# Second mixer's latents projected without their norm, which enters in the heads; q's norm in the exponential; c loaded as 32 rows

## Chip, cores and metric

One core of one Trainium2 chip runs the whole kernel in one launch. The metric is device time in microseconds (us). The kernel before takes 999.2 us, the median of three runs (997.95 to 1000.5).

## What is computed

The reference is a trunk of two layers for one sequence of 256 tokens with 1024 features, all in fp32. Each layer is a gated feed-forward network (FFN, 2816 hidden), an attention mixer, and another FFN. Each of these normalizes its input and shifts, scales and gates it with vectors that come from the conditioning vector c. The second mixer projects to a small latent for q (384 wide) and one for k and v (256 wide, and 32 more for a shared rotary part of k), normalizes the latents, and projects them up to 16 heads of 96 (64 without and 32 with rotary position). Cut to what matters here:

```python
def rms_norm(x, g):
    return x * lax.rsqrt(jnp.mean(x * x, axis=-1, keepdims=True) + EPS) * g

def mla_shared_kv(...):
    hs = modulate(rms_norm(x, kv_norm_g), shift, scale)   # shift, scale from silu(c)
    ckv_kpe = hs @ w_dkv
    ckv = rms_norm(ckv_kpe[..., :256], kv_a_norm_g)
    kpe = ckv_kpe[..., 256:]
    k_nope = (ckv @ w_uk).reshape(B, S, 16, 64)
    v = (ckv @ w_uv).reshape(B, S, 16, 64)
    k = concatenate([k_nope, kpe for every head])
    k = rms_norm(k, k_g)                    # over 96, then rope on the last 32
    return k, v

def mla_attention(h, ...):
    q = (rms_norm(h @ w_dq, q_a_norm_g) @ w_uq).reshape(B, S, 16, 96)
    q = rms_norm(q, q_g)                    # over 96, then rope on the last 32
    o = causal_attention(q, k, v, scale=96 ** -0.5)
    return o.reshape(B, S, 1024) @ w_o
```

A root-mean-square norm divides each row by a number of its own. A row of the latent that is not divided by it gives a row of q (or k, v) that is too large by that number, and the norm over the head divides it out again, up to the small constant EPS, which must then be multiplied by the square of that number.

## The kernel before

The 256 tokens are two tiles of 128, called t. Every fp32 product with a weight is three matmuls: the weight is split into a rounded part hi (written by ScalarE, L634) and a rest lo (written by VectorE, L635), and so is the activation (`split_evac`, L779 and L780); the products hi·hi, hi·lo and lo·hi are summed in PSUM (`mm3`, L764 to L766). Weights come by DMA on SyncE's queue in one long stream.

The stages run in this order: `first` (the start and the first 768 hidden rows of the first FFN, until about 52 us), the rest of the first FFN, the first mixer (about 240 to 340), two FFNs, the second mixer `mla` (about 704 to 804), and the last FFN. The conditioning weights (16 tiles of 512 KB for each norm, and as many halves for the gates) are multiplied with c on VectorE (L645 for shifts and scales, L683 for gates) all through the kernel; L645 multiplies a tile of weights with `c_b`, which is c, after SiLU, repeated on all 128 partitions.

The order of the instructions on each engine is not that of the program. The class `Order` records all instructions with their dependencies, gives each a cost from formulas (`duration`) and each buffer pool its number of buffers, places the instructions by list scheduling in a simulated time, and then fixes the order found, engine by engine. `later(us, fn)` in the program text postpones the emission of a piece of work by that much estimated TensorE time; constants such as `LAT_WAIT` are such waits. So a change of one instruction, cost or constant can move instructions anywhere in the kernel.

The start. The queue of ScalarE loads c (as 128 partitions by 8 columns, L1523) and then `cols` (biases, gains and other columns, L1524). SyncE's queue loads x and then the first weights. ScalarE applies SiLU to c (L1536). Eight matmuls (L1541, sixteen passes in the profile) repeat c on all partitions: the stationary operand is a column of c broadcast to 128 columns, the moving one is the identity; the result is copied in two halves to `c_b` (L1542). For the norm of x, VectorE takes the square sum of tile 0 (L1558), ScalarE that of tile 1 (L1555), GpSimd takes the power −0.5 (L801), and ScalarE puts it on a diagonal (L1562), by which TensorE transposes and scales x at once (L1572). With the shift and scale from L645, ScalarE makes z (L1589), which is split to h, and the main matmuls follow (L1609 to L1611), for k from 0 to 7 with the weights rounded by L1600 and L1601. Matmuls of zeros into the accumulators (L1548) open them and run before all of this.

The second mixer. For each t, TensorE projects to the q latent and to the k-v latent. `lat_norm_T` (L1376) takes ScalarE's square sum of a latent from PSUM (L1379), adds EPS on VectorE (L1381), takes the power −0.5 on GpSimd (L1383), multiplies the latent from PSUM by that and by the gain on VectorE (L1384), and later transposes it on TensorE (L1389) and splits it to `qlT` or `ckT` (L779, L780). Then four groups g of four heads: `proj` projects the latent to q, `head_rstd` (L1103) takes square (ScalarE, L1106), sum by head (VectorE, L1109), add (L1110) and power (GpSimd, L1111), VectorE multiplies (L1474, `qn`), and the rotary part follows. k and v are done the same way (L1488, L1489, L1491). `to_T` (L1449) transposes q and k on TensorE, four heads at a time for each t (L1454), into a tile of the pool `ps_tr`, which has three PSUM banks and also serves the latents' transposes, the scores, the transposed probabilities and the output; ScalarE copies each with the gain (L1455). `attention` then makes scores in three units: a mask by a matmul (L1018) with the products of q and k on top (L1020), the negated maximum on VectorE (L1030), the exponential on ScalarE (L1041), reciprocal and multiplication on VectorE (L1046, L1047), transposes of the probabilities (L1056) with ScalarE's copies (L1058), and the products with v (L1076). `out_proj` closes the mixer. The pool `ps_ada` has one PSUM bank, which the gates' sums use.

Of the kernel before, what the change touches and what calls it, by code (L numbers as in the profile page):

```python
# [21 lines left out]
P = 128  # L22
D = 1024
KD = D // P
# [42 lines left out]
AV_WAIT = 2.6  # L67
LAT_WAIT = 5.0
G_WAIT = 2.6
# [59 lines left out]
def lay_out(v):  # L129
# [54 lines left out]
WAKE = 100.0  # L184
SWITCH = 95.0
TABLE = 1280.0
RATE = 330.0
# [59 lines left out]
class Order:  # L247
# [120 lines left out]
    def place(self, need):  # L368
# [68 lines left out]
        while placed < n:  # L437
# [90 lines left out]
def trunk(ctx: ExitStack, tc: tile.TileContext, a: dict, out: bass.AP):  # L528
# [88 lines left out]

    all_cols = cp.tile([P, 3 * NK + NT + 4 + 2 * RO], F32, name="cols")
    cact = cp.tile([P, KD], F32, name="cact")
    places = {}  # L620
    c0 = 3 * NK
    for name, n in (("pos", NT), ("moba_q", 1), ("moba_k", 1), ("q", 1), ("q_pe", RO), ("k", 1), ("k_pe", RO)):
        places[name] = all_cols[:, c0:c0 + n]
        c0 += n
    cols = all_cols[:, :3 * NK].rearrange("p (i c) -> p i c", i=3)
    m_cols = cp.tile([P, 2, NK], F32, name="m_cols")
# [375 lines left out]

    def attention(ap, g, qTs, kTs, vs, bias, oT, state, after_s=None):

# [5 lines left out]
        def scores():  # L1010
# [14 lines left out]
            for (t, es), ps3 in zip(UNITS, banks):  # L1025
                nk = P * (t + 1)
                s3 = ap.tile([P, 512], F32, tag="w", name=nm("s"), bufs=5).rearrange("p (e k) -> p e k", k=nk)
                mx = small([P, 4], "mx")
                if bias is None:
                    nc.vector.tensor_reduce(mx[:, :len(es)], ps3, axis=AX.X, op=ALU.max, negate=True)  # L1030
                else:
                    for i, e in enumerate(es):
                        s2, ps2 = [x[:, i, :].rearrange("p (b c k) -> p b c k", c=P // NB, k=NB) for x in (s3, ps3)]
                        nc.vector.tensor_tensor_reduce(s2, ps2, bias(t, e), 1.0, 3.0e38,
                                                       op0=ALU.add, op1=ALU.min, accum_out=mx[:, i:i + 1])
                ss.append(s3)
                mxs.append(mx)
            for u, (t, es) in enumerate(UNITS):
                sm = small([P, 4], "sm")
                for i in range(len(es)):  # L1040
                    nc.scalar.activation(ss[u][:, i, :], (banks if bias is None else ss)[u][:, i, :], AF.Exp,  # L1041
                                         bias=mxs[u][:, i:i + 1], scale=1.0 if bias is None else -1.0,
                                         accum_out=sm[:, i:i + 1])
# [58 lines left out]

    def head_rstd(ap, src, n, d, extra=None):  # L1103
# [3 lines left out]
        nh = n // (d if extra is None else DH)  # L1107
        v, v2, r = [small([P, 2 * GH], g)[:, :nh] for g in ("hv", "hv2", "hr")]
        nc.vector.tensor_reduce(v, sq.rearrange("p (h d) -> p h d", h=nh), axis=AX.X, op=ALU.add)  # L1109
        nc.vector.tensor_scalar(v2, v, EPS if extra is None else extra, None, op0=ALU.add)  # L1110
        nc.gpsimd.tensor_tensor(r, v2, mhalf[:, :nh], op=ALU.pow)  # L1111
        return r
# [262 lines left out]

    def lat_norm_T(ap, src, n, gain, lat, t):  # L1376
        y = ap.tile([P, 512], F32, tag="w", name=nm("ly"), bufs=5)[:, :n]
        s = small([P, 1], "ssq0")
        nc.scalar.activation(y, src, AF.Square, scale=n ** -0.5, accum_out=s)  # L1379
        v = small([P, 1], "var")  # L1380
        nc.vector.tensor_scalar(v, s, EPS, None, op0=ALU.add)  # L1381
        r = small([P, 1], "rstd")
        nc.gpsimd.tensor_tensor(r, v, mhalf[:, 0:1], op=ALU.pow)  # L1383
        nc.vector.scalar_tensor_tensor(y, src, r, gain, op0=ALU.mult, op1=ALU.mult)  # L1384

        def fin():
# [6 lines left out]
            lat[2].add(t)  # L1393
        later(LAT_WAIT, fin)

    def mla(h, hs, after):
        with ExitStack() as st:
# [10 lines left out]
            qlT = [one([P, QL // P, S], f"qlT{i}", F32R) for i in range(2)] + [set()]  # L1408
            kpr, spe = [], []

            NV = KVL + RO
            pls = [[], []]
            for t in range(NT):
                for i, (src, n) in ((1, (h, QL)), (0, (hs, NV))):
# [5 lines left out]
                    if i:  # L1420
                        lat_norm_T(ap, ps[:, :QL], QL, ga_q, qlT, t)
                        continue
                    lat_norm_T(ap, ps[:, :KVL], KVL, ga_kv, ckT, t)
                    kpe = one([P, 1, RO], f"kpe{t}")
# [24 lines left out]
            def to_T(g, kind, nat, gcol, then):  # L1449
                dst = ap.tile([QK, GH, S], F32, tag=kind + "T", name=nm(kind + "T"))  # L1450
                for t in range(NT):
                    pt = tr_tile()
                    for e in range(GH):
# [6 lines left out]
                if len(then) == 2:  # L1460
                    qT, kT = then["q"], then["k"]
                    attention(ap, g, lambda e, t: qT[:, e, t * P:(t + 1) * P], lambda e, n: kT[:, e, :n],
                              lambda e, kb: vs[g][:, kb, e * DH:(e + 1) * DH], None, oT, state)

            vs = {}
            for g in range(NG):
                then = {}
                pq = nextw()
                qn = ap.tile([P, NT, GH, QK], F32, tag="qn", name=nm("qn"), bufs=1)
                for t in range(NT):  # L1470
# [3 lines left out]
                    nc.vector.tensor_tensor(qn[:, t], heads(pq_), r[:, :, None].to_broadcast([P, GH, QK]), op=ALU.mult)  # L1474
                pes = qn[:, :, :, DH:]
# [7 lines left out]
                for t in range(NT):  # L1483
                    ps = proj(t, ckT, pkv, KVL // P, 2 * GH * DH)
                    until(lambda: state.get("Tk", 0) >= g)
                    pk_ = ps[:, :GH * DH]
                    r = head_rstd(ap, pk_, GH * DH, QK, extra=spe[t])
# [9 lines left out]
    def first(units):  # L1497
# [5 lines left out]
        with ExitStack() as st:  # L1503
            fp = st.enter_context(tc.tile_pool(name="fp", bufs=1))
            zeros = fp.tile([P, P], BF16, name="zeros")
            nc.vector.memset(zeros, 0.0)
            wt = [[splitp.tile([P, D], F32, tag=g, name=nm("adaw")) for g in ("hi", "lo")] for _ in range(KD)]
            cuts = (0, FIRST_A, n1)
# [13 lines left out]
            with ranked(0):  # L1522
                nc.scalar.dma_start(cact, a["c"])  # L1523
                nc.scalar.dma_start(all_cols, a["cols"])  # L1524
# [10 lines left out]
            with ranked(0):  # L1535
                nc.scalar.activation(cact, cact, AF.Silu)  # L1536
                for i in range(2):
                    pt = tr_tile()
                    for j in range(4):
                        k = 4 * i + j  # L1540
                        nc.tensor.matmul(kslice(pt, j), cact[:, k:k + 1].to_broadcast([P, P]), ident, start=True, stop=True)  # L1541
                    nc.scalar.activation(c_b[:, i * 512:(i + 1) * 512], pt, AF.Copy)  # L1542
            ps_x = [tr_tile(), ps_ada.tile([P, 512], F32, tag="ada", name=nm("tr"))]
            accs = [tr_tile() if f >= 4 else mm_tile() for f in range(B1)]


            for f in range(B1):
                nc.tensor.matmul(accs[f], zeros, zeros[:, None].to_broadcast([P, 4, P]), start=True, stop=False)  # L1548
            diag, rs, y, fill = [], [], {}, 10
# [113 lines left out]
```

## Time and profile before

| | before |
|---|---|
| median of the runs | 999.2 us (997.95, 999.2, 1000.5) |
| profiled execution, its own time | 999.38 us |
| span of its instructions | 997.6 us |
| mean granted TensorE clock | 0.997 |
| instructions | 15253 |
| HBM read | 255.34 MB, 260 GB/s over the span |

The span is the time from the first to the last instruction that the profiler saw; 1.8 us of the execution's own time lie outside it. PE is TensorE's matmul stream and PEld its loading of stationary operands beside it, DVE is VectorE, ACT is ScalarE, POOL is GpSimd and SP is SyncE; an engine's name with a q is its queue of DMA issues. A row of the timeline gives start and duration in us, then engine, line and operation, with the operands out<-in; in square brackets stands how long the engine had been idle before and what released it. A row of a group gives busy time and the mean of one in ns, and behind the second bar the idle time before them. The length of a matmul includes its way through the array: where matmuls follow each other, their starts, not their lengths, tell the price.

### The profile page before, as it was taken

To read this page: it belongs to the slowest core of one execution; us is meant where nothing else is said; L and a number is where in the kernel's file an instruction comes from. 1 tells how busy PE (TensorE), PEld (TensorE's weight loads), DVE (VectorE), ACT (ScalarE), POOL (GpSimd) and SP (SyncE) were. 2 spreads that over 40 slices of the span, in tenths; PEclk is the share of its full clock that TensorE was granted. 3 is DMA by queue.
4 is the path that set the end of the run, shared out by engine and by line. 5 is a ranking of instruction groups with operands and counts; after the bars stand their busy time and mean duration, and the time that the engine had idled before them with its cause. 6 is when DMAs were issued, how large, how long until landed. Compare 5 with 4: busy or idle time off the path is not lost.

```text
span 997.6 us, 15253 instructions
## 1 busy us (share of the span) xinstructions
PE 982.7 (99%) x5570; PEld 839.4 (84%) x5570; DVE 845.7 (85%) x1430; ACT 629.9 (63%) x1173; POOL 88.8 (9%) x124
## 2 busy tenths in 40 slices
PE   7999999999999999999999999999999999999998
PEld 6988888888888788888888888888888878888886
DVE  6999999898999899999789999964998789777542
ACT  5689565378766976665367666643879696667421
POOL 1012020022231100000000000000143010000000
PEclk8999999999999999999999999999999999999999
DMA  9978889898786689988979988862343468544530
GB/s 366 404 244 286 312 314 353 311 339 336 261 317 233 226 303 327 340 292 302 371 297 330 353 308 307 286 236 102 106 154 127 169 230 290 199 169 170 230 127 22
DMA packets 53371, 260.53 MB, mean 261 GB/s; under 512 B 6320, under 2 KB 6832, under 8 KB 35120
## 3 DMA queue, kind: packets, MB, share of 16 engines
q1 hardware_dynamic: 51696, 255.93, 70.3%
q0 software_dynamic: 1024, 3.17, 1.1%
q8 instruction: 44, 0.72, 0.3%
q10 hardware_dynamic: 576, 0.45, 0.2%
q14 instruction: 31, 0.25, 0.1%
HBM read 255.34 MB, written 4.19 MB: 260 GB/s over the span
## 4 chain that ended last, share of the span: by engine, by line
PE 91%; DVE 3%; issue 2%; DMA 2%; ACT 1%; POOL 1%; POOLq 0%; ACTq 0%; DVEq 0%
PE mm L964 23%; PE mm L764 15%; PE mm L765 15%; PE mm L766 15%; PE mm L972 12%; PE at L1020 2%; DMA bias_d<-bt 1%; PE at L1076 1%; PE at L1056 1%; PE tr L814 1%; PE mm L1609 1%; DVE lo L635 1%; PE mm L1610 1%; PE mm L1611 1%; PE tr L1454 1%
## 5 line engine op out<-in xcount | busy, mean ns | idle before, releaser
L635 DVE TENSOR_TENSOR lo<-raw,hi 128x1024 fp32r<-128x1024 f32 (+3 forms) x312 | 369.0, 1199 | 69.6 <-ACT hi L634 64.2
L634 ACT ACTIVATE hi<-raw 128x1024 fp32r<-128x1024 f32 (+3 forms) x312 | 319.6, 1038 | 154.3 <-PE mm L766 117.4
L964 PE MATMUL mm<-h,hi 128*128 128x512 f32 x1120 | 289.2, 394 | 1.1 <-DVE g L903 0.8
L964 PEld LDWEIGHTS mm<-h,hi 128*128 128x128 f32 x1120 | 199.5, 189 | 36.5 <-DVE g L903 1.6
L972 PEld LDWEIGHTS mm<-h,lo 128*128 128x128 f32 x1120 | 155.3, 190 | 12.1
L972 PE MATMUL mm<-h,lo 128*128 128x256 f32 x1120 | 162.0, 282 | 0.0
L645 DVE CUSTOM_DVE_ANT_0 adaw<-adaw,c_b,cols 128x1024 f32<-128x1024 f32 x112 | 141.9, 1280 | 2.0 <-DMA adaw<-in_ada_dram 2.0
L764 PE MATMUL mm<-hi,gh 128*128 128x512 f32 x352 | 137.4, 390 | 0.0
L765 PE MATMUL mm<-lo,gh 128*128 128x512 f32 x352 | 137.1, 390 | 0.0
L766 PE MATMUL mm<-hi,gl 128*128 128x512 f32 x352 | 137.1, 389 | 0.0
L764 PE MATMUL mm<-hi,h 128*128 128x512 f32 (+1 forms) x240 | 94.7, 401 | 0.1
L765 PE MATMUL mm<-lo,h 128*128 128x512 f32 (+1 forms) x240 | 93.6, 393 | 0.0
L766 PE MATMUL mm<-hi,h 128*128 128x512 f32 (+1 forms) x240 | 91.6, 390 | 1.0 <-DVE h L780 1.0
L766 PEld LDWEIGHTS mm<-hi,gl 128*128 128x128 f32 x352 | 66.1, 188 | 13.7
L764 PEld LDWEIGHTS mm<-hi,gh 128*128 128x128 f32 x352 | 66.1, 188 | 13.5
L765 PEld LDWEIGHTS mm<-lo,gh 128*128 128x128 f32 x352 | 66.1, 188 | 13.3
L683 DVE SCALAR_TENSOR_TENSOR acc<-adaw,cact,acc 128x1024 f32<-128x1024 f32 x48 | 61.4, 1279 | 0.3
L766 PEld LDWEIGHTS mm<-hi,h 128*128 128x128 f32 x240 | 45.1, 188 | 9.9 <-DVE h L780 1.2
L764 PEld LDWEIGHTS mm<-hi,h 128*128 128x128 f32 x240 | 45.0, 188 | 8.7 <-ACT h L779 0.6
L801 POOL TENSOR_TENSOR rstd<-ssq,mhalf 128x1 f32<-128x1 f32 x12 | 15.3, 1276 | 411.9 <-DVE ssq L796 344.4
L765 PEld LDWEIGHTS mm<-lo,h 128*128 128x128 f32 x240 | 45.2, 188 | 7.9 <-issue 0.2
L779 ACT ACTIVATE gh<-g 128x256 fp32r<-128x256 f32 x76 | 31.4, 413 | 28.7 <-DVE g L906 25.9
(233 smaller groups left out, 1253.8 us busy)
## 6 DMA issues: line engine op xcount, KB each, us to landing
raw<-in_w_dram SPq DMA_DIRECT2D x142, 1024.0 KB, 6.0
adaw<-in_ada_dram SPq DMA_DIRECT2D x160, 512.0 KB, 5.6
raw<-in_w_dram SPq DMA_DIRECT2D x12, 512.0 KB, 3.6
raw<-in_first_dram SPq DMA_DIRECT2D x7, 512.0 KB, 9.0
raw<-in_w_dram SPq DMA_DIRECT2D x6, 576.0 KB, 3.8
bias_d<-bt SPq DMA_DIRECT2D x12, 256.0 KB, 4.6
bg<-bias_d POOLq DMA_DIRECT2D x4, 768.0 KB, 6.8
raw<-in_first_dram SPq DMA_DIRECT2D x10, 256.0 KB, 9.0
```

Source lines behind the costliest of these rows:

```text
L634: nc.scalar.activation(hi, src, AF.Copy)
L635: nc.vector.tensor_tensor(lo, src, hi.bitcast(F32), op=ALU.subtract)
L645: nc.vector.tensor_tensor_reduce(wt, wt, c_b, 1.0, cols[:, i, c:c + 1], op0=ALU.mult, op1=ALU.add, accum_out=m_cols[:, i, c:c + 1])
L683: nc.vector.scalar_tensor_tensor(acc, ada_tile(j, k), cact[:, k:k + 1], acc, op0=ALU.mult, op1=ALU.add)
L764: nc.tensor.matmul(ps, lh, rh, start=start, stop=False)
L765: nc.tensor.matmul(ps, lh, rl, start=False, stop=False)
L766: nc.tensor.matmul(ps, ll, rh, start=False, stop=stop)
L779: nc.scalar.activation(hi, ps, AF.Copy)
L801: nc.gpsimd.tensor_tensor(r, stats[t], mhalf[:, 0:1], op=ALU.pow)
L964: nc.tensor.matmul(ps[i], w[0], hs[2], start=k == 0, stop=False)
L972: nc.tensor.matmul(ps[i][:, S:], w, hk_, start=False, stop=k == KD - 1)
L1020: nc.tensor.matmul(ps3[:, i, :], qTs(e, t), kTs(e, nk), start=bias is not None, stop=bias is not None or i == len(es) - 1)
```

## The change

It has five parts and some retuning of the planner's constants.

1. c comes as 8 rows of 128 numbers, padded with zeros to 32 rows, into the first 32 partitions of a tile whose other rows VectorE zeroes; the columns of c (for the gates) ride in `cols`, which has 246 columns instead of 238, and get a SiLU of their own. The matmuls that repeat c now take a column of the identity as the stationary operand and the tile of c as the moving one. On ScalarE the new SiLU stands between the SiLU of the rows and the first copy to `c_b`, and the square sum of x between the two copies.
2. Three matmuls of zeros more (two in place of one for the accumulators 1 to 3); six of them now stand ahead of the matmuls that repeat c (four before).
3. The latents are multiplied by their gain only, straight from PSUM, and transposed; their square sum is taken beside that. The add and the power go from their path. VectorE makes `epq`, (s + EPS)·EPS, for q, and `w`, s + EPS, for k; GpSimd makes `rkv`, w to the power −0.5. In the heads, `epq` takes the place of EPS, the rotary part of k and its share of the sum are multiplied by powers of w, and the copy of v takes `rkv` as its scale.
4. q is not multiplied by its norm. ScalarE copies it for groups 0 and 1, VectorE for groups 2 and 3; the norm's factor `rq` multiplies the negated maximum (one small VectorE multiplication per unit, 12 in all) and is the exponential's scale operand.
5. `to_T` transposes into the one bank of `ps_ada`.

`LAT_WAIT` goes from 5 to 3, and the planner counts matmuls that it places before 5.6 us twice. The number of matmuls that carry weights is the same.

```diff
-LAT_WAIT = 5.0
+LAT_WAIT = 3.0
...
-    out["c"] = v["c"].reshape(KD, P).T
-    more = [pos.view(np.float32).reshape(NT, P).T]
+    out["c"] = np.concatenate([v["c"].reshape(KD, P), np.zeros((32 - KD, P), np.float32)])
+    more = [v["c"].reshape(KD, P).T, pos.view(np.float32).reshape(NT, P).T]
...
+COLD = 5600.0
...
+                if t < COLD:
+                    occ, dur = 2 * occ, dur + occ
...
                 mx = small([P, 4], "mx")
                 if bias is None:
                     nc.vector.tensor_reduce(mx[:, :len(es)], ps3, axis=AX.X, op=ALU.max, negate=True)
+                    nc.vector.tensor_tensor(mx[:, :len(es)], mx[:, :len(es)], scale[:, t, es[0]:es[-1] + 1], op=ALU.mult)
...
-                                         bias=mxs[u][:, i:i + 1], scale=1.0 if bias is None else -1.0,
+                                         bias=mxs[u][:, i:i + 1], scale=scale[:, t, e:e + 1] if bias is None else -1.0,
...
-    def lat_norm_T(ap, src, n, gain, lat, t):
+    def lat_T(ap, src, n, gain, lat, t):
         y = ap.tile([P, 512], F32, tag="w", name=nm("ly"), bufs=5)[:, :n]
+        nc.vector.tensor_tensor(y, src, gain, op=ALU.mult)
+        junk = ap.tile([P, 512], F32, tag="sq", name=nm("sq"), bufs=1)[:, :n]
         s = small([P, 1], "ssq0")
-        nc.scalar.activation(y, src, AF.Square, scale=n ** -0.5, accum_out=s)
-        v = small([P, 1], "var")
-        nc.vector.tensor_scalar(v, s, EPS, None, op0=ALU.add)
-        r = small([P, 1], "rstd")
-        nc.gpsimd.tensor_tensor(r, v, mhalf[:, 0:1], op=ALU.pow)
-        nc.vector.scalar_tensor_tensor(y, src, r, gain, op0=ALU.mult, op1=ALU.mult)
+        nc.scalar.activation(junk, src, AF.Square, scale=n ** -0.5, accum_out=s)
...
+                        s = lat_T(ap, ps[:, :QL], QL, ga_q, qlT, t)
+                        epq.append(one([P, 1], f"epq{t}"))
+                        nc.vector.tensor_scalar(epq[t], s, EPS, EPS, op0=ALU.add, op1=ALU.mult)
...
+                    s = lat_T(ap, ps[:, :KVL], KVL, ga_kv, ckT, t)
+                    w = one([P, 1], f"w{t}")
+                    nc.vector.tensor_scalar(w, s, EPS, None, op0=ALU.add)
+                    rkv.append(one([P, 1], f"rkv{t}"))
+                    nc.gpsimd.tensor_tensor(rkv[t], w, mhalf[:, 0:1], op=ALU.pow)
...
-                    nc.vector.tensor_scalar(s, s, EPS, None, op0=ALU.add)
+                    nc.vector.tensor_scalar(s, s, EPS, w, op0=ALU.add, op1=ALU.mult)
...
+                    nc.vector.tensor_scalar(kr[:, 0, :], kr[:, 0, :], w, rkv[t], op0=ALU.mult, op1=ALU.mult)
...
             def to_T(g, kind, nat, gcol, then):
-                    pt = tr_tile()
+                    pt = ps_ada.tile([P, 512], F32, tag="ada", name=nm("tr"))
...
-                    r = head_rstd(ap, pq_, GH * QK, QK)
-                    nc.vector.tensor_tensor(qn[:, t], heads(pq_), r[:, :, None].to_broadcast([P, GH, QK]), op=ALU.mult)
+                    if g < 2:
+                        nc.scalar.activation(qn[:, t], heads(pq_), AF.Copy)
+                    else:
+                        nc.vector.tensor_copy(qn[:, t], heads(pq_))
+                    head_rstd(ap, pq_, GH * QK, QK, extra=epq[t], out=rq[:, t])
...
-                    nc.scalar.activation(v[:, t, :], ps[:, GH * DH:], AF.Copy)
+                    nc.scalar.activation(v[:, t, :], ps[:, GH * DH:], AF.Copy, scale=rkv[t])
...
+            c8 = fp.tile([P, P], F32, name="c8")
+            for p in (32, 64):
+                nc.vector.memset(c8[p:2 * p], 0.0)
...
-                nc.scalar.dma_start(cact, a["c"])
+                nc.scalar.dma_start(c8[:32], a["c"])
...
-                nc.scalar.activation(cact, cact, AF.Silu)
+                nc.scalar.activation(c8[:32], c8[:32], AF.Silu)
...
-                        nc.tensor.matmul(kslice(pt, j), cact[:, k:k + 1].to_broadcast([P, P]), ident, start=True, stop=True)
+                        nc.tensor.matmul(kslice(pt, j), ident[:, k:k + 1].to_broadcast([P, P]), c8, start=True, stop=True)
...
+            with ranked(3):
+                nc.scalar.activation(cact, cact, AF.Silu)
...
-                nc.tensor.matmul(accs[f], zeros, zeros[:, None].to_broadcast([P, 4, P]), start=True, stop=False)
+                for i in range(2 if 1 <= f < 4 else 1):
+                    nc.tensor.matmul(accs[f], zeros, zeros[:, None].to_broadcast([P, 4, P]), start=i == 0, stop=False)
```

More of the change, by code (lines that the diff above doesn't have):

```diff
@@ L616, in trunk @@
     pos_f = a["positions"].rearrange("o s -> (o s)")
-    all_cols = cp.tile([P, 3 * NK + NT + 4 + 2 * RO], F32, name="cols")
-    cact = cp.tile([P, KD], F32, name="cact")
+    all_cols = cp.tile([P, 3 * NK + KD + NT + 4 + 2 * RO], F32, name="cols")
     places = {}
     c0 = 3 * NK
-    for name, n in (("pos", NT), ("moba_q", 1), ("moba_k", 1), ("q", 1), ("q_pe", RO), ("k", 1), ("k_pe", RO)):
+    for name, n in (("c", KD), ("pos", NT), ("moba_q", 1), ("moba_k", 1), ("q", 1), ("q_pe", RO), ("k", 1), ("k_pe", RO)):
         places[name] = all_cols[:, c0:c0 + n]
         c0 += n
-    cols = all_cols[:, :3 * NK].rearrange("p (i c) -> p i c", i=3)
+    cols, cact = all_cols[:, :3 * NK].rearrange("p (i c) -> p i c", i=3), places["c"]
     m_cols = cp.tile([P, 2, NK], F32, name="m_cols")
@@ L1039, in scores @@
                 sm = small([P, 4], "sm")
-                for i in range(len(es)):
+                for i, e in enumerate(es):
                     nc.scalar.activation(ss[u][:, i, :], (banks if bias is None else ss)[u][:, i, :], AF.Exp,
-                                         bias=mxs[u][:, i:i + 1], scale=1.0 if bias is None else -1.0,
+                                         bias=mxs[u][:, i:i + 1], scale=scale[:, t, e:e + 1] if bias is None else -1.0,
                                          accum_out=sm[:, i:i + 1])
@@ L1101, in out_proj, with head_rstd @@
                     after(t)
-    def head_rstd(ap, src, n, d, extra=None):
+    def head_rstd(ap, src, n, d, width=None, extra=EPS, out=None):
         sq = ap.tile([P, 512], F32, tag="sq", name=nm("sq"), bufs=1)[:, :n]
         nc.scalar.activation(sq, src, AF.Square, scale=d ** -0.5)
-        nh = n // (d if extra is None else DH)
-        v, v2, r = [small([P, 2 * GH], g)[:, :nh] for g in ("hv", "hv2", "hr")]
+        nh = n // (width or d)
+        v, v2 = [small([P, 2 * GH], g)[:, :nh] for g in ("hv", "hv2")]
+        r = small([P, 2 * GH], "hr")[:, :nh] if out is None else out
         nc.vector.tensor_reduce(v, sq.rearrange("p (h d) -> p h d", h=nh), axis=AX.X, op=ALU.add)
-        nc.vector.tensor_scalar(v2, v, EPS if extra is None else extra, None, op0=ALU.add)
+        nc.vector.tensor_scalar(v2, v, extra, None, op0=ALU.add)
         nc.gpsimd.tensor_tensor(r, v2, mhalf[:, :nh], op=ALU.pow)
@@ L1394, in lat_norm_T @@
         later(LAT_WAIT, fin)
+        return s
     def mla(h, hs, after):
```

13 lines of the change are left out of this document (6 added, 7 removed).

## The prediction

> **What bounds the kernel now.** I read the page first: busy time by engine and the chain of waits.
>
> ```profile
> PE 982.7 (99%) x5570; PEld 839.4 (84%) x5570; DVE 845.7 (85%) x1430; ACT 629.9 (63%) x1173; POOL 88.8 (9%) x124
> PE 91%; DVE 3%; issue 2%; DMA 2%; ACT 1%; POOL 1%; POOLq 0%; ACTq 0%; DVEq 0%
> ```
>
> TensorE is busy 982.7 of 997.6 us and carries 91% of the chain. The change takes no matmul of weight out, so it can only fill holes in TensorE or shorten the time before its stream starts. Where the holes lie is read from the busy times by stretch (PE, PEld, DVE, ACT, POOL, then clock, DMA share, GB/s):
>
> ```profile
> 11.69:18.51 6.82, 5.97 (x32) 5.91 (x33) 5.93 (x10) 4.69 (x9) 0.91 (x17) 0.50 1.03 405
> 18.51:22.00 3.49, 3.49 (x31) 3.49 (x30) 3.38 (x7) 2.47 (x4) 0.00 (x0) 1.00 1.05 411
> 16.00:50.00 34.00, 34.00 (x278) 34.00 (x277) 33.90 (x62) 21.91 (x36) 0.00 (x0) 0.96 1.03 404
> 52.00:704.00 652.00, 650.79 (x3648) 551.58 (x3647) 588.24 (x966) 413.44 (x744) 54.43 (x73) 1.00 0.81 294
> 704.00:733.00 29.00, 26.09 (x152) 22.79 (x151) 27.80 (x81) 22.77 (x61) 7.99 (x7) 1.00 0.41 114
> 733.00:804.00 71.00, 70.97 (x464) 60.50 (x463) 61.34 (x133) 57.41 (x140) 19.79 (x17) 1.00 0.39 141
> 804.00:998.00 194.00, 188.79 (x974) 160.66 (x973) 125.13 (x172) 104.95 (x179) 1.66 (x3) 1.00 0.51 185
> ```
>
> Three places matter. Before 16 us the stream has not started. From 16 to 50 us VectorE is full (33.90 of 34) and the DMA engines are full (share 1.03). In 704–733, where the latents are made, TensorE misses 2.91 us. From 52 to 704 it misses only 1.2 us and DMA has room (0.81), so whatever is won at the start is carried to the end. The 5.2 us missing after 804 lie outside the edits.
>
> **The change, part 1: the start.** The timeline of the first stage:
>
> ```profile
> 0.74 0.40 ACTq L1523 DMA_DIRECT2D cact<-in_c_dram  x1
> 1.02 1.89 PE L1548 MATMUL mm<-zeros 128*128 128x512 bf16 x4 [1.02 <-DVE zeros L1506]
> 4.46 1.22 DVE L1558 CUSTOM_DVE_ANT_0 raw<-x 128x1024 f32<-128x1024 f32 x1 [2.17 <-DMA x<-in_x_dram]
> 4.67 0.21 ACT L1536 ACTIVATE cact<-cact 128x8 f32<-128x8 f32 x1 [1.73 <-DMA cact<-in_c_dram]
> 5.03 3.57 PE L1541 MATMUL tr<-ident,cact 128*128 128x128 f32 x16 [2.12 <-ACT cact L1536]
> 6.44 0.15 DVE L1232 TENSOR_SCALAR cols<-cols 128x1 f32<-128x1 f32 x1 [0.74 <-DMA cols<-in_cols_dram]
> 8.63 0.60 ACT L1542 ACTIVATE c_b<-tr 128x512 f32<-128x512 f32 x1 [0.93 <-PE tr L1541]
> 9.13 1.05 ACT L1555 ACTIVATE raw<-x 128x1024 f32<-128x1024 f32 x1
> 10.30 0.15 DVE L1556 TENSOR_SCALAR ssq<-ssq 128x1 f32<-128x1 f32 x1 [3.71 <-ACT raw L1555]
> 10.37 1.28 DVE L645 CUSTOM_DVE_ANT_0 adaw<-adaw,c_b,cols 128x1024 f32<-128x1024 f32 x1
> 10.53 1.52 POOL L801 TENSOR_TENSOR rstd<-ssq,mhalf 128x1 f32<-128x1 f32 x1 [4.18 <-DVE ssq L1556]
> 12.09 0.40 ACT L1562 ACTIVATE diag<-ident,rstd 128x128 f32<-128x128 f32 x1 [1.54 <-POOL rstd L801]
> 14.59 0.78 PE L1609 MATMUL mm<-h,whi 128*128 128x256 f32 x2
> ```
>
> The chain to the first main matmul: c lands (4.67), SiLU, the broadcast of c by matmuls (3.57), two copies on ScalarE, the square sum of the second half of x behind them (9.13), add on VectorE (10.30), power on GpSimd, diag, transposes, z, h, 14.59: 4.29 us from the add.
>
> c as 32 rows of 512 bytes: the trace has no such load. It lands no later than the 4 KB of before in 128 rows of 32 bytes (gain 0). At the other end the broadcast cannot start before the zero matmuls ahead of it, now six instead of four: 1.02 + 6 × 1.89/4 = 3.86. So it starts between 3.86 and 4.9; I take 4.1, near the first, as the same bytes come in a quarter of the rows. Its first half is there 1.8 later (3.57/2), at 5.9.
>
> The new SiLU on c as columns stands on ScalarE ahead of the first copy and needs cols, which lands at 6.44 and carries 8 columns more (246 for 238). Queued behind that wait are both copies and the square sum, and behind those VectorE's weight products. If cols keeps its 6.44, the copy starts at 6.65; if it moves up with c's packets, which are ahead of it on the same queue, at 5.9. I take 6.0. Then: copy 0.60 to 6.6, square sum and hand-over 1.17 (9.13 to 10.30), add at 7.8 against 10.30; second copy from 7.75 (its half of the broadcast is there at 4.1 + 3.57 = 7.67) to 8.35, first weight product at 8.4 against 10.37. Gain at the head: 2.0 for the products, 2.5 for the add; with cols at 6.44 it is 1.3 and 1.85, with the broadcast at 3.86 and cols no hindrance 2.3 and 2.85. The first main matmul follows the add by 4.29: 12.1 to 12.3, as z also needs both products (8.4 + 2 × 1.28 = 11.0; z stood at 13.4 before, behind power, diag and transposes, which are 2.5 earlier too).
>
> How much is left at the end of the stage? VectorE is full, so it moves up with its first product. But the transfers are full as well. The last weights of this stage, by the queue's timeline, the line's time to landing and their use:
>
> ```profile
> 34.04 0.96 SPq L1520 DMA_DIRECT2D raw<-in_first_dram  x2
> DMA to landing us min/median/max: 6.0/9.0/10.4
> 46.48 1.22 DVE L1601 TENSOR_TENSOR wlo<-raw,whi 128x1024 fp32r<-128x1024 f32 x1
> ```
>
> Issued by 34.7 and landing 9.0 later they are there at 43.7; the rounding on ScalarE takes about 1.0, so the split at 46.48 can come some 1.8 earlier, a little more where the issue moves up too. I take **−1.9** (range −0.4, if landings at 10.4 decide: 45.1 + 1.0 = 46.1, to −2.8). The two zeroing instructions at VectorE's head lie in its idle time before x (2.17, its row above); the first broadcast waits for them too, but at 4.1 they are done; uncovered, two of VectorE's tiny instructions would cost about 0.3 (0.15 by the row at 6.44).
>
> TensorE is nearly as full as VectorE in this stage (278 matmuls in 34.00 us, 0.122 each), so its cold stretch counts. By the first two stretches it runs at half clock from 11.69 to 18.51. From 14.59 that loses half of 3.9 us, 2.0. With the start at 12.2 and the clock's rise at 18.51 as before it would lose 3.15, 1.15 more, and gain 2.4 − 1.15 = 1.25 in all; with the rise one half of that stretch earlier (15.1) it loses 1.45 and gains 2.95. Busy from 12.2 instead of 14.59, the rise should come earlier; −1.9 lies between the two. The Trainium skill ("TensorE: Matmul & The Clock Gate", Part 1) calls the window free-running and about 3.4 us long. The trace agrees in the length (6.82 is two of them); by the page the choice between those two values could differ from run to run.
>
> **Part 2: the latents.** The holes in TensorE, by the timeline, and the groups of that stage:
>
> ```profile
> 708.29 0.45 PE L766 MATMUL mm<-hi,h 128*128 128x384 f32 x1 [0.97 <-DVE h L780]
> 725.19 0.44 PE L766 MATMUL mm<-hi,qlT 128*128 128x384 f32 x1 [0.32 <-DVE qlT L780]
> 727.65 0.45 PE L764 MATMUL mm<-hi,qlT 128*128 128x384 f32 x1 [0.63 <-ACT qlT L779]
> 732.02 0.50 PE L764 MATMUL mm<-hi,ckT 128*128 128x512 f32 x1 [0.76 <-ACT ckT L779]
> ```
> ```profile
> L1379 ACT ACTIVATE ly<-mm 128x384 f32<-128x384 f32 x2 | 0.9, 469 | 0.0
> L1381 DVE TENSOR_SCALAR var<-ssq 128x1 f32<-128x1 f32 x4 | 0.6, 148 | 0.0
> L1383 POOL TENSOR_TENSOR rstd<-var,mhalf 128x1 f32<-128x1 f32 x4 | 4.2, 1050 | 13.6 <-DVE var L1381 13.5
> L1384 DVE SCALAR_TENSOR_TENSOR ly<-mm,rstd,ga_q 128x384 f32<-128x384 f32 x2 | 1.2, 618 | 0.4 <-POOL rstd L1383 0.4
> L1474 DVE TENSOR_TENSOR qn<-mm,hr 128x384 f32<-128x384 f32 x8 | 4.4, 551 | 0.0
> ```
>
> The first hole is not touched. The other three wait for latents: 0.32 + 0.63 + 0.76 = 1.71, and about 0.1 each for refilling the pipe: 2.0. Per latent 0.47 + 0.15 + 1.05 = 1.7 us of square, add and power leave the path, each more than any of the holes, so all can close; at most 2.0.
>
> VectorE's load there (27.80 of 29) decides whether they do. Removed: four adds of 0.15, and four products qn of 0.55 (groups 0 and 1, whose copies go to ScalarE at about 0.47 by the square of the same size). Added: four tiny instructions on the latents' sums and two on kr, 0.15 each by the add, and one such multiply for each of the 12 score tiles. Net −0.6 −2.2 +0.9 +1.8 = −0.1 over the mixer, but −0.6 −1.1 +0.9 = −0.8 up to the first scores, with one group's products. VectorE's own idle time there is 1.2, so some hole of VectorE's making stays: I let 1.6 of 2.0 come. Two powers on GpSimd instead of four are nothing: nobody waits for them but kr and v (GpSimd is busy 7.99 of 29).
>
> **Part 3: the heads.** Transposes of q and k now pass through one PSUM bank instead of three. Before (timeline, then groups):
>
> ```profile
> 747.75 1.04 PE L1454 MATMUL tr<-ident,qn 128*96 128x128 f32 x8
> 749.68 1.28 ACT L1455 ACTIVATE kT<-tr,cols 96x512 f32<-96x512 f32 x2
> ```
> ```profile
> L1455 ACT ACTIVATE qT<-tr,cols 96x512 f32<-96x512 f32 x8 | 5.1, 685 | 0.3 <-PE tr L1454 0.3
> L1041 ACT ACTIVATE s<-at,mx 128x256 f32<-128x256 f32 x16 | 7.6, 485 | 0.3 <-issue 0.3
> L832 ACT ACTIVATE y<-tr,m_cols 128x128 f32<-128x128 f32 x8 | 3.3, 447 | 0.2 <-PE tr L814 0.2
> L779 ACT ACTIVATE h<-y 128x128 fp32r<-128x128 f32 x4 | 1.1, 305 | 0.0
> ```
>
> A group's four batches took 747.75 to 750.96, 3.2 us. Through one bank each turn is 1.04/2 + 0.69 = 1.21, four are 4.8: 1.6 more, and 1.0 on top where two Exps (0.49 each) stand between two turns on ScalarE, which works in order: 2.6. What hides it is the next group's projections on TensorE (70.97 of 71 busy in 733–804); the first group, with least work ready, is where cover may fail. I take 0 here, between nothing and 4 × 2.6; what would be late next are the group's scores, and behind them its Exps and p. The multiply of the maximum (0.15) delays each first Exp; the wait for it is 0.15, hidden likewise.
>
> Exp takes its scale from memory now: 32 of them. L832 with two such operands takes 0.14 more than L779 with none, so about 0.07 each, 2.3 us of ScalarE, which idles 13.6 in 733–804. I take 0; in the open, 2.3. (The eight copies of v gain such an operand as well: 0.6, in the same idle time.) Against the change speaks a sentence of the Trainium skill ("ScalarE: Activation LUTs", What ACT_TABLE_LOAD costs): each pointer operand adds about 93 ns; by it, as an estimate, the price would be 3.0 instead of 2.3.
>
> The orders of all engines are planned anew (the latents' delay in the plan goes from 5 to 3, and the plan now counts the first matmuls double); elsewhere TensorE is full, so ±1.0 around 0.
>
> **Sum**, for the profiled run (span 997.6, 1.8 around it, 999.4; the median of the runs is 0.2 lower): −1.9 −1.6 = −3.5. On the median: 999.2 − 3.5 = **995.7**.
>
> **Rivals.** (a) Both gains in full: −2.8 and −2.0, and 0.6 of the 0.8 by which VectorE is lighter before the scores shows too: 999.2 − 5.4 = 993.8. For it: VectorE never waits in 16–50, so all of a head start shows; against it the transfers at 1.03. (b) The holes come back as waits for VectorE (only its lighter load of 0.8 shows), and cols and the transfers hold the start to −0.4: 999.2 − 1.2 = 998.0. For it 27.80 of 29 and 6.44. (c) Slower: the single bank decides. Its point: the fourth evacuation ends after the next scores are due, TensorE having no projections left. Out-projections cover the last group, so three groups × 2.6 = 7.8, less 3.5: 1003.5. For it: ScalarE is in order, 57.41 of 71; against it: no idle on TensorE there now, so work is at hand. (d) Exp's scale on the path of the softmax: −3.5 + 2.3: 998.0. For it: ScalarE's Exps are what the scores' banks wait for; against it, the idle 13.6.
>
> **How the numbers follow.** 0.3% is 3.0 us, about what a measurement of this kernel tells from no change; so faster means under 996.2. Forecast 0.50 (own range 994.2–997.2; 0.40 faster, 0.10 same), (a) 0.18, faster; (b) 0.12 (0.02 faster, 0.09 same, 0.01 slower); (c) 0.14 (0.01 same, 0.13 slower); (d) 0.06 (0.04 same, 0.02 slower). Faster 0.60, same 0.24, slower 0.16. The range leaves out (c) and the last of (a): 992.8 to 999.6.
>
> **What would show it.** Right: the first main matmul starts at 11.8–12.8, the first weight product at 8.0–9.1; the first big FFN matmul about 2 earlier; no wait for qlT or ckT over 0.3 on TensorE. Wrong: a wait of TensorE for qT, kT or s over 1 us in any group (c); the wait of ScalarE for cols reaching 6.4 (b); new holes in stages that the edits do not touch (the re-planned order).

## The result: slower by 0.2%

| | before | after |
|---|---|---|
| median of 13 runs | 999.38 us (997.75 to 1000.5) | 1001.12 us (1000.05 to 1002.2) |
| ratio after/before | | 1.0022 (95%: 1.0014 to 1.0029) |
| profiled execution, span | 999.38, 997.6 | 1001.43, 999.7 |

The forecast was 995.7, a gain of 3.5; the change costs about 2. The lines of the two profiles are compared stage by stage. First the start, in the timeline of the changed kernel (its lines are 2 to 25 higher):

```profile
0.74 0.42 ACTq L1545 DMA_DIRECT2D c<-in_c_dram  x1
3.74 0.31 ACT L1558 ACTIVATE c<-c 32x128 f32<-32x128 f32 x1 [0.80 <-DMA c<-in_c_dram]
4.19 3.53 PE L1563 MATMUL tr<-c,ident 128*128 128x128 f32 x16
6.27 0.21 ACT L1566 ACTIVATE cols<-cols 128x8 f32<-128x8 f32 x1 [2.22 <-DMA cols<-in_cols_dram]
8.04 0.15 DVE L1581 TENSOR_SCALAR ssq<-ssq 128x1 f32<-128x1 f32 x1 [1.61 <-ACT raw L1580]
8.27 0.55 POOL L803 TENSOR_TENSOR rstd<-ssq,mhalf 128x1 f32<-128x1 f32 x1 [1.99 <-DVE ssq L1581]
8.52 1.28 DVE L647 CUSTOM_DVE_ANT_0 adaw<-adaw,c_b,cols 128x1024 f32<-128x1024 f32 x1 [0.33 <-ACT c_b L1564]
12.26 0.74 PE L1634 MATMUL mm<-h,whi 128*128 128x256 f32 x4 [1.68 <-ACT h L781]
```

The first main matmul comes at 12.26 instead of 14.59. ScalarE waits for cols (6.27) as feared, but the matmuls that repeat c run meanwhile. By busy times (stretch, PE, PEld, DVE, ACT, POOL, clock, DMA share, GB/s) and by ScalarE's waits, again of the changed kernel:

```profile
12.00:20.00 8.00, 7.74 (x63) 7.67 (x64) 7.80 (x14) 4.95 (x9) 0.00 (x0) 1.00 1.03 404
20.00:30.00 10.00, 9.42 (x75) 8.77 (x74) 9.09 (x17) 5.46 (x11) 0.00 (x0) 1.00 1.03 406
```
```profile
ACT whi L1625 <- DMA raw<-in_first_dram: 10.7, 6, 2.4
```

The half clock of before has gone (1.00 from 12 us on), so TensorE is at first about 4 us ahead. From 20 to 30 it idles 0.58, where before it was full, and ScalarE waits 10.7 us in all for weights: the transfers set the pace. What is left at the end of the stage shows in the first matmul of the next part, before and after:

```profile
52.27 2.00 PE L964 MATMUL mm<-h,hi 128*128 128x512 f32 x8
```
```profile
50.31 2.00 PE L966 MATMUL mm<-h,hi 128*128 128x512 f32 x8
```

2.0 us. Now the mixer, by busy times, before and then after:

```profile
700.00:740.00 40.00, 37.09 (x215) 32.42 (x214) 36.65 (x103) 31.54 (x80) 12.29 (x12) 1.00 0.42 122
740.00:756.00 16.00, 16.00 (x114) 13.71 (x113) 13.91 (x35) 14.41 (x37) 5.26 (x5) 1.00 0.45 159
```
```profile
700.00:740.00 40.00, 38.89 (x225) 34.29 (x225) 38.15 (x108) 34.26 (x86) 10.12 (x9) 1.00 0.47 145
740.00:756.00 16.00, 13.97 (x97) 11.88 (x95) 12.29 (x33) 14.25 (x34) 4.00 (x4) 0.89 0.47 173
```

The holes at the latents are closed (1.8 us of TensorE's idle time less before 740), and 2.03 us open behind the first group's scores, where TensorE was full. The clock falls there too (0.89). The timeline of the changed kernel at that place:

```profile
740.37 2.78 PE L1023 MATMUL at<-kT,qT 96*128 96x128 f32 x16
741.46 0.69 DVE L1033 TENSOR_REDUCE mx<-at 128x4 f32<-128x512 f32 x1 [0.41 <-PE at L1023]
742.19 0.16 DVE L1034 TENSOR_TENSOR mx<-mx,rq 128x4 f32<-128x4 f32 x1
742.42 1.28 ACT L1045 ACT_TABLE_LOAD   x1 [0.92 <-DVE mx L1034]
742.99 0.60 PE L1468 MATMUL tr<-ident,qn 128*96 128x128 f32 x4
743.72 0.46 ACT L1045 ACTIVATE s<-at,mx,rq 128x128 f32<-128x128 f32 x1
744.79 1.22 DVE L637 TENSOR_TENSOR lo<-raw,hi 128x1024 fp32r<-128x1024 f32 x1
746.17 0.18 DVE L1050 RECIPROCAL rs<-sm 128x4 f32<-128x4 f32 x1 [0.16 <-ACT s L1045]
747.10 0.69 ACT L1469 ACTIVATE qT<-tr,cols 96x512 f32<-96x512 f32 x1
747.22 0.63 PE L1060 MATMUL at<-ident,s 128*128 128x128 f32 x4 [2.03 <-DVE rs L1050]
747.84 0.94 PE L1468 MATMUL tr<-ident,qn 128*96 128x128 f32 x4
```

Read from the bottom: the second batch of q's transposes (747.84) needs the one bank, which ScalarE empties at 747.10 only, behind seven Exps; so TensorE's next work is the probabilities (747.22), which wait for Exps and reciprocal. Before, TensorE had the same projections and 16 transposes of q and k (747.75 to 749.86) to do in between; here it has 4. The Exps begin 3.35 us after the first product of the scores; before they began 2.18 after it:

```profile
743.09 1.06 PE L1020 MATMUL at<-kT,qT 96*128 96x128 f32 x8
743.98 1.28 ACT L1041 ACT_TABLE_LOAD   x1
744.18 0.69 DVE L1030 TENSOR_REDUCE mx<-at 128x4 f32<-128x512 f32 x1
745.27 0.37 ACT L1041 ACTIVATE s<-at,mx 128x128 f32<-128x128 f32 x1
```

The load of the exponential's table now stands behind the multiplied maximum (0.92 idle), where it used to run beside the maximum. The traces show what differs. Before, the first Exp itself carries the wait for VectorE, and the load ran ahead of it. In the changed kernel the Exp carries a wait for TensorE, and a separate instruction at 742.38, which waits for VectorE, stands ahead of the load.

### The profile page after: what moved, and what is told of

It reads as the page before. It is cut to its first block, busy times and chain, and to the rows that moved or that the text cites. A ratio compares the mean times of both kernels' runs of the same rounds, so it can differ in the third digit from the quotient of the medians.

```text
span 999.7 us, 15297 instructions
## 1 busy us (share of the span) xinstructions
PE 985.5 (99%) x5570; PEld 838.4 (84%) x5573; DVE 842.4 (84%) x1442; ACT 630.7 (63%) x1178; POOL 83.1 (8%) x122
## 3 DMA queue, kind: packets, MB, share of 16 engines
HBM read 255.36 MB, written 4.19 MB: 260 GB/s over the span
## 4 chain that ended last, share of the span: by engine, by line
PE 74%; issue 11%; DVE 7%; DMA 4%; ACT 2%; POOL 1%; SPq 0%; ACTq 0%; POOLq 0%; DVEq 0%
PE mm L966 20%; PE mm L766 12%; PE mm L767 12%; PE mm L768 12%; PE mm L974 10%; DVE lo L637 2%; PE at L1023 2%; DMA raw<-in_first_dram 2%; DMA raw<-in_w_dram 1%; PE at L1080 1%; PE at L1060 1%; PE tr L1468 1%; PE tr L816 1%; POOL rstd L803 1%; DVE acc L685 1%
## 5 line engine op out<-in xcount | busy, mean ns | idle before, releaser
L974 PEld LDWEIGHTS mm<-h,lo 128*128 128x128 f32 x1120 | 155.2, 190 | 12.3 <-DVE lo L637 0.4
L685 DVE SCALAR_TENSOR_TENSOR acc<-adaw,cols,acc 128x1024 f32<-128x1024 f32 x48 | 61.6, 1283 | 0.7 <-DMA adaw<-in_ada_dram 0.6
L904 ACT ACTIVATE g<-mm 128x256 f32<-128x256 f32 x70 | 26.2, 375 | 44.0 <-PE mm L974 43.6
L803 POOL TENSOR_TENSOR rstd<-ssq,mhalf 128x1 f32<-128x1 f32 x12 | 13.1, 1088 | 409.9 <-DVE ssq L798 368.9
```

What stands on the lines that cost most here:

```text
L685: nc.vector.scalar_tensor_tensor(acc, ada_tile(j, k), cact[:, k:k + 1], acc, op0=ALU.mult, op1=ALU.add)
L803: nc.gpsimd.tensor_tensor(r, stats[t], mhalf[:, 0:1], op=ALU.pow)
L904: nc.scalar.activation(x, ps[:, S:], AF.Copy)
L974: nc.tensor.matmul(ps[i][:, S:], w, hk_, start=False, stop=k == KD - 1)
```

## The experiments

The kernels were run in five rounds each beside the kernel before on the same chip; ratios are to that kernel, whose median was 998.99 to 999.49 on the different chips. "Order" kernels carry a list of instruction numbers for each engine instead of the planner's result; the planner's own lists of two kernels, cut at a planned time and joined, make it:

```diff
-        for ks in self.work_out()[1].values():
+        for ks in pinned.values():
```

| kernel | ratio to before (95%) | median us |
|---|---|---|
| changed kernel | 1.0022 (1.0014 to 1.0029) | 1001.12 |
| start_only | 0.9999 (0.9990 to 1.0007) | 999.33 |
| start_pinned | 0.9981 (0.9972 to 0.9990) | 996.85 |
| replan_only | 1.0019 (1.0010 to 1.0028) | 1000.86 |
| after_pinned | 1.0002 (0.9994 to 1.0011) | 998.86 |
| mla_only | 1.0038 (1.0025 to 1.0050) | 1003.17 |
| bank3 | 1.0005 (0.9996 to 1.0014) | 999.08 |
| bank3_pinned | 1.0005 (0.9996 to 1.0014) | 999.03 |
| bank1_before | 1.0018 (1.0009 to 1.0027) | 1001.06 |
| earlyexp | 1.0019 (1.0010 to 1.0027) | 1000.57 |
| bank_early | 0.9987 (0.9978 to 0.9996) | 997.98 |
| lat_only | 0.9991 (0.9982 to 1.0000) | 998.09 |
| q_only | 1.0006 (0.9998 to 1.0015) | 999.77 |

**The start and the order of the rest.** start_only is the kernel before with parts 1 and 2 of the change and the planner's double count.

> The kernel before with the start's edits alone (c as 32 rows, zero matmuls, planner's double count before 5.6 us). Theory: in the changed kernel TensorE had lost 2.1 us less than before by 60 us, and nothing of that depends on the second mixer; so this kernel is 2 to 2.5 us faster than before (about 997). Rival, the start's gain is lost again to the transfers and the re-planned order: within 0.8 us of before.

It is level with before. Yet its first matmul of the next part came as early as the changed kernel's, within 0.4 us. Two kernels tell where the gain went.

> The start's edits alone, as in start_only, but every instruction that the plan of the kernel before places after 16 us stands in exactly that plan's order (the order written into the kernel). Theory: the start is worth about 1.8 us at its end (first matmul of the next part at 50.6 against 52.3) and start_only lost that again only because the planner drew another order for the rest (in all re-planned kernels TensorE loses some 1.2 us more at 200-220 and 0.7 at 520). So 997.2 to 998.0 here. Rival, transfers or chance take it back whatever the order: 999 to 999.8.

> The kernel before, without any edit of an instruction: its own order up to 16 us of the plan, and from there the order that the plan of start_only has. Theory (the drawn order costs what start_only lost): 1.2 to 2.2 us slower than before, with TensorE's extra lost time at 200-220 and 520. Rival (the order is worth nothing by itself; start_pinned's gain has another reason): within 0.7 us of before.

start_pinned is 1.9 us faster than before (0.9981; its theory gave the start about 1.8) and replan_only, which edits nothing but the order after 16 us, 1.9 us slower. So the start is worth what was forecast for it, and the other order that the planner drew behind it costs as much. TensorE's waits from 52 to 700 us, in replan_only and then in start_pinned (who waited for whom: us in total, times, longest; lines are about 228 higher for the list):

```profile
PE tr L1041 <- ACT y L1036: 0.3, 1, 0.3
PE tr L1507 <- DVE qn L1487: 0.3, 1, 0.3
PE mm L993 <- DVE h L1007: 0.2, 1, 0.2
```
```profile
PE mm L1194 <- DVE u L1133: 0.3, 1, 0.3
```

A handful of small waits, of transposes for a norm's scaled x or for q, and of a split. The first and the last sit at the same places in the changed kernel. The busy times of two of the stretches, replan_only and then before, show TensorE missing 0.36 and 0.35 us. Counted by the start of the same weight matmul in both traces, replan_only is 0.9 us ahead of before at 200 us, 0.2 behind at 220, 0.6 at 340, and 1.4 behind at 600:

```profile
200.00:222.00 22.00, 21.64 (x96) 16.76 (x95) 20.75 (x27) 14.93 (x28) 5.70 (x7) 1.00 0.92 336
510.00:530.00 20.00, 19.65 (x92) 15.67 (x91) 17.72 (x27) 16.24 (x34) 3.00 (x2) 1.00 0.91 333
```
```profile
200.00:222.00 22.00, 22.00 (x101) 17.86 (x101) 21.31 (x28) 15.78 (x29) 5.48 (x7) 1.00 0.93 336
510.00:530.00 20.00, 20.00 (x96) 16.35 (x95) 19.40 (x32) 18.28 (x39) 3.00 (x2) 1.00 0.92 344
```

So 1.1 us go at the first place and 0.8 between 340 and 600, more than the idle time; at the first place three matmuls of replan_only start 0.37, 0.50 and 0.53 us after the one ahead of them, none of before more than 0.35. The 0.9 ahead at 200 is not the order's: the trace of before has a wait of 0.79 for g at 119 that replan_only's lacks. Under the same old order after_pinned and lat_only (below) have that wait too, start_pinned and q_only do not, so single traces of one order differ by about 1 us.

**The changed kernel with the old order between.**

> The changed kernel, but from 16 us to 680 us of the plan in the order of the kernel before; the start and all from the second mixer on as the changed kernel has them. Theory (the other order outside the edits costs 1.5 to 2 us): 999.2 to 999.8 against 1001.1 of the changed kernel. Rival (everything is in the mixer): 1000.7 to 1001.3.

2.0 us less than the changed kernel, as the theory expected. Beside start_pinned, which differs only from 680 us on, it is 2.1 slower (1.0002 against 0.9981). So the change is three sums: start −1.9, order +1.9, mixer +2.1, each known to about 1 us by the intervals.

**The mixer alone.**

> The changed kernel with its start put back to the one before: the second mixer's edits alone. Theory: they cost about 4 us (TensorE's lost time from 732 on is 6 us more than before, its holes at the latents 2 us less), so 1003 to 1004. Rival, the loss in the mixer comes from the other order that the earlier start brought: within 1 us of before.

Slower by 3.8 us in five runs, which is the mixer and the drawn order together. Their mean clocks are 0.993 to 0.998, so a part of it may be the clock.

**The bank.** bank3 and bank3_pinned undo this line, bank1_before makes it alone:

```diff
-                    pt = ps_ada.tile([P, 512], F32, tag="ada", name=nm("tr"))
+                    pt = tr_tile()
```

> The changed kernel with one line undone: the transposes of q and k go back to the pool of three banks. Theory (the single bank makes the chain of transposes and copies): the 2 us hole at 745 and the lost time to 756 go, 996 to 997.5. Rival (the first group's softmax is late by itself: the multiplied maximum and the table load behind it, the longer Exps): the hole stays, within 1 us of the changed kernel.

> The changed kernel with q and k through three banks, all up to 690 us of the plan in the changed kernel's order. The part of the bank without the drawn order elsewhere. Theory (the bank costs the chain of turns after the hole, the hole itself stays): 0.8 to 1.5 us faster than the changed kernel. Rival (bank3's gain was the order elsewhere): equal to it within 0.5.

> The kernel before with that one line alone: q and k through the single bank, all else as before. Theory (single bank): 2 to 4 us slower than before, with waits of TensorE's transposes for ScalarE's copies. Rival: less than 1 us.

Both kernels with three banks are 1.7 us faster than the changed one, the pinned one too, so this is the bank, with the order that the planner draws for the mixer, and not the order elsewhere. bank3 fell short of its forecast, and bank3_pinned went a little beyond its own: the hole stays, by TensorE's waits at 740 to 757 in bank3_pinned, now for a bank that an Exp has to free:

```profile
PE tr L1696 <- ACT s L1273: 1.7, 1, 1.7
```

bank1_before is 1.8 us slower, just under the 2 to 4 expected. Its waits in the mixer show the chain of turns (a probability's transposes behind q's copy):

```profile
PE at L1056 <- ACT qT L1455: 0.7, 1, 0.7
PE at L1056 <- DVE s L1047: 0.3, 1, 0.3
```

A wait of TensorE of 1.6 us for the norm at 210 is also in its trace, outside the edit. The instructions of every engine stand there in the order of before; VectorE waits for conditioning weights that land late in this execution:

```profile
208.16 1.28 DVE L683 SCALAR_TENSOR_TENSOR acc<-adaw,cact,acc 128x1024 f32<-128x1024 f32 x1 [1.67 <-DMA adaw<-in_ada_dram]
```

So this wait is not drawn order. Whether the other runs have it is not known.

A part of the 1.7 is the clock. Take the moments at which the same number of TensorE's loads of stationary operands is still to come, in before and in another trace. From 700 to 850 us the changed kernel loses 2.9 us against before by this count; its trace has 3.4 us of half clock behind the hole (last section). The trace of earlyexp (below), with the single bank, a hole of 1.8 and the full clock, loses 1.1, that of bank3 0.25, that of bank1_before 1.9. The runs of earlyexp, none with a mean clock under 0.999, are 1.4 above bank3's. So in the changed mixer the bank costs about 1 us without the clock.

**The table load.** earlyexp and bank_early put a tiny exponential ahead:

```diff
+            if bias is None and g == 0:
+                nc.scalar.activation(small([P, 4], "sm")[:, 0:1], mhalf[:, 0:1], AF.Exp)
```

> The changed kernel in its own order, with one tiny exponential of a constant put on ScalarE just ahead of the second mixer's first exponential, so that the table load does not wait for the multiplied maximum (0.92 us of idle time in the trace). Theory (the hole of 2.0 us at 745 is the first group's softmax arriving late): the hole shrinks by 0.8 to 1.0, the time by about 1, 999.9 to 1000.4. Rival (the single bank or VectorE's reciprocal sets the hole): no change.

> The changed kernel with the order of the kernel before up to 680 us, three banks, and the tiny exponential ahead of the mixer's first. Theory (what remains of the mixer's cost over after_pinned, 998.9, is the bank, 1.7, and the table load behind the maximum, up to 1): 996.0 to 997.2, and the hole at 745 about 0.7 against 1.8 with three banks. Rival (the load is no limit once the banks are there): 997.0 to 997.6 with the hole at 1.7.

earlyexp missed: 0.3 us, inside the interval. The load did move (741.67, first Exp 743.07 against 743.72), but the hole shrank from 2.0 to 1.8 only, because the reciprocal stands behind a 1.22 us split of weights on VectorE. In bank_early the load could not move, as ScalarE was busy until 739.19, 1.9 us after the first product of the scores at 737.25; the hole is 1.6, as the rival said, and its time, a little over the rival's range, lies 1.5 under after_pinned, which the bank explains alone.

**Latents and q's norm apart**, both with the new start, the old order up to 680 us and three banks:

> The new start, the order of the kernel before up to 680 us, and of the second mixer's edits only the latents without their norm (q multiplied by its norm on VectorE as before, Exp's scale a constant, three banks). Beside start_pinned, which has the same start and order and the old mixer. Theory (the holes at the latents were worth 2 us and came back at 745 because the first group's softmax was made longer): the hole at 745 stays under 0.5 us, the time is 1 to 2 us under start_pinned's 996.85: 994.9 to 995.9. Rival (TensorE comes to the scores 2 us earlier and then waits for the same softmax whatever its length): the hole is 1.5 to 2, 996.5 to 997.2.

> The same start and order, the latents normalised as before, three banks; q's norm in the exponential alone. Theory: the first group's Exps come 1.2 us later behind the table load and take 0.6 us longer, with TensorE no earlier than before: a hole of 1 to 1.8 at 745, 997.9 to 998.7 against 996.85. Rival (VectorE's lighter load pays for it): 996.4 to 997.2.

TensorE's waits from 700 to 812 in lat_only, then in q_only:

```profile
PE tr L1694 <- DVE kn L1729: 0.6, 1, 0.6
PE mm L993 <- ACT h L1008: 0.5, 1, 0.5
PE mm L993 <- ACT v L1731: 0.5, 1, 0.5
...
PE tr L1694 <- ACT s L1271: 0.2, 1, 0.2
```
```profile
PE tr L1690 <- ACT s L1273: 1.7, 1, 1.7
PE mm L994 <- ACT h L1009: 1.1, 2, 0.7
PE mm L994 <- ACT qlT L1009: 0.6, 1, 0.6
```

The hole behind the scores belongs to q's norm in the exponential: 1.7 with it even where the latents are as before, 0.2 without it. Counted from the first product of the scores, the first Exp comes 3.37 us later in q_only (739.87, 743.24) and 2.47 in lat_only (740.48, 742.95); q_only's table load waits 0.61 for the multiplied maximum, lat_only's does not wait. The first six Exps take 3.07 and 2.50 us, three and two of them of the longer form. These differences, 0.90 and 0.57, make 1.47 of q_only's wait of 1.7, which ends with the sixth Exp. q_only is 2.5 us over start_pinned, more than the 1.0 to 1.9 of its theory. lat_only's hole is gone as the theory said, but its time is not: 1.0 us over start_pinned instead of 1 to 2 under it. Its trace has new waits in place of the old (kn, v, h): by the count of loads it gains 0.85 from 700 to 745 and has lost that at 756. Both edits together with three banks (bank_early) are 0.6 over start_pinned, so the two prices do not add. Each of these mixers has its own drawn order, so differences of about 1 us between them are not settled by these runs.

start_pinned beats both kernels: 996.85, 0.9981 of before.

## Why the prediction was wrong

- **The start, −1.9: right.** The broadcast began at 4.19 (taken: 4.1), the first product at 8.52 (8.4), the add at 8.04 (7.8), the first main matmul at 12.26 (12.1 to 12.3); the next part came 2.0 earlier and start_pinned gained 1.9. The transfers are the cap that the step named. Two gains inside it were not foreseen and fed the cap only: the clock stayed full, and GpSimd's power took 0.55 instead of 1.52.
- **"The orders of all engines are planned anew; elsewhere TensorE is full, so ±1.0 around 0": the first step that failed.** The order alone is +1.9 (replan_only).
- **The latents, −1.6: closed and given back.** The holes of 0.32, 0.63 and 0.76 went, and TensorE came to the first product of the scores 2.7 us earlier (0.8 of it brought along from before 700), to wait 2.03 behind them. The step looked at VectorE's load and not at what is late next: between the first group's scores and its probabilities TensorE has the same projections as before and fewer transposes to fill the time. That the closed holes moved there is not shown, as q_only has the wait without them.
- **The single bank, 0: the second step that failed.** "The first group is where cover may fail" was the right place, and zero the wrong value: undoing the line gains 1.7, about 1 of it without the clock, and making it alone costs 1.8. Rival (c) named it; its price of 7.8 for three groups was too high. Where the loss falls differs: by the count of loads the changed kernel's trace loses 1.65 more than bank3's from 745 to 756, its half clock included, and 0.6 from there to 850; bank1_before loses 1.7 of its 1.9 after 756.
- **Exp's scale, 0 on the path: the third.** The groups before and after:

```profile
L1041 ACT ACTIVATE s<-at,mx 128x128 f32<-128x128 f32 x16 | 5.8, 365 | 1.4 <-DVE mx L1030 1.4
```
```profile
L1045 ACT ACTIVATE s<-at,mx,rq 128x256 f32<-128x256 f32 x16 | 9.1, 577 | 0.4 <-DVE mx L1034 0.4
L1045 ACT ACTIVATE s<-at,mx,rq 128x128 f32<-128x128 f32 x16 | 7.2, 458 | 2.0 <-DVE mx L1034 2.0
```

Each Exp is 0.093 longer at 128 and 0.092 at 256 (485 before), so 32 of them 3.0 us, not the 2.3 from the rows chosen. The Trainium skill ("ScalarE: Activation LUTs", What ACT_TABLE_LOAD costs) has 93 ns for a pointer operand; these rows agree. In the first group the lengthening of six of them, about 0.6 us, lies in the open by q_only. The multiplied maximum, priced as a hidden 0.15, held a table load of 1.28 back by 0.92 (in q_only by 0.61, and the first Exp came 0.90 later than in lat_only). No run multiplies the maximum without making the scale an operand, so which of the two put the wait ahead of the load stays open.

The three failed steps are worth 1.9 (order) and 1.6 + 2.1 (a mixer at −1.6 that came out at +2.1); the forecast of −3.5 with them gives +2.1, and 1.0022 is +2.2.

## What to carry to other kernels

Where a planner fixes the order of everything, an edit is two changes: measure it once with the old order kept outside the edit, or its worth is hidden behind that of a new order. Before a hole ahead of a serial chain is closed, ask what fills the time in that chain, and whether it shares a buffer with the chain. Where an instruction first has to load a table, see whether a wait comes to stand ahead of the load: the price is the overlap that the load loses, not the length of the small operation waited for.

## What the hardware showed unexpectedly

The wait at 745 took the clock with it. The busy times and the granted clock of the changed kernel:

```profile
744.60:748.00 3.40, 1.37 (x10) 0.84 (x9) 3.17 (x8) 3.40 (x14) 0.76 (x1) 1.00 0.36 89
748.50:751.50 3.00, 3.00 (x16) 2.50 (x16) 2.90 (x9) 2.71 (x6) 0.00 (x0) 0.51 0.56 235
```

After 3.4 us in which TensorE was busy for 1.37, it ran at half clock for about 3.4 more. The trace of after_pinned shows the same behind its hole of 2.0; those of mla_only, with a hole of 2.0 too, and of earlyexp, with 1.8, do not. The mean clock of a run shows that there were such stretches but not where (the changed kernel's trace has a second at its end): of its 13 runs six have 0.997 or 0.998 (mean 1001.6 us) and seven 1.000 (mean 1000.6). A hole of 2 us may thus cost 1.0 us more by these means, or up to 1.7, half of 3.4, in the trace where it happens. What decides it is not shown.

GpSimd's power on one column took 0.55 us after 1.99 us of idleness and 1.52 after 4.18, both at the start of these two kernels.
